# Gate and up products of a SwiGLU block with the weights stationary, in eight of eleven groups

## The chip, the cores and the metric

The program runs on one core of a Trainium2 chip. The time is that of one execution on the device, in microseconds (us). A core has five engines that matter here: TensorE (PE; the loads of its stationary operand are listed apart, as PEld), VectorE (DVE), ScalarE (ACT), GpSimd (POOL) and SyncE (SP), whose queue issues the DMAs. The metric is the median of several executions; the profile is of one further execution.

## The reference, cut to what matters

Two layers over 256 tokens of width 1024. Each layer is a feed-forward block (FFN), a mixer, and another FFN, each followed by a layer norm, in float32:

```python
def swiglu(x, w_gate, w_up, w_down):
    return (jax.nn.silu(x @ w_gate) * (x @ w_up)) @ w_down
...
for l in range(DEPTH):
    x = layer_norm(ALPHA * x + 0.5 * swiglu(x, ffn1_gate[l], ffn1_up[l], ffn1_down[l]), ln_g[l, 0], ln_b[l, 0])
    ...
    x = layer_norm(ALPHA * x + mix, ln_g[l, 1], ln_b[l, 1])
    x = layer_norm(ALPHA * x + 0.5 * swiglu(x, ffn2_gate[l], ffn2_up[l], ffn2_down[l]), ln_g[l, 2], ln_b[l, 2])
```

The hidden width of an FFN, `D_FF`, is 2816. There are four FFNs in all, and the change is in them.

## The kernel before, in words

**Precision.** A float32 operand is split into two float32r tiles, a high part (names ending in h) and the rest (ending in l): ScalarE casts, VectorE subtracts (`halves`, lines 101 and 102). A product is then three matmuls, high by high, high by low, low by high (`mm3`, lines 95 to 97), added up in one PSUM bank. In the profile a matmul is written `out<-moving,stationary`.

**Tiles.** The 256 tokens are two halves of 128 (`hf`). x of each half is kept transposed, as eight blocks of 128 by 128 (`xth`, `xtl`, one pair per half from a pool of three buffers), written by `Transposed.part` after a layer norm. The hidden width is cut into `NG` = 11 groups of `GW` = 256. The weights of a group come in four blocks of 128 by 1024, each holding two rows of blocks (kt) with 256 gate and 256 up columns, through two rings in SBUF: `w` with eight buffers and `x` with two. The down weights come in two blocks a group, through a ring `d` of six. A DMA brings each block as it is, `halves` splits it.

**One group.** `G(g, hf)` multiplies one half of the tokens with all weights of the group: x blocks are stationary, 512 weight columns move, 8 kt by 3 matmuls into one PSUM bank (`gu`), tokens on the partitions. `gate` takes silu of the gate columns on ScalarE (`sil`) and multiplies with the up columns on VectorE (`hn`). `T` transposes `hn`, two matmuls of 128 columns against the identity (line 355), and splits the result from PSUM into `hth` and `htl`. `D(g, hf)` multiplies these with the down weights: 4 `mm3` of 512 columns into two banks (`acc`) that add up over all eleven groups.

**Order.** TensorE's order is written out by hand: what is called first is recorded first. `T` is put off by a counter (`later`) that counts calls of `mm3`, six on from the gate, so that its two matmuls fall inside a later product; if `D` is called before its `T` was, `T` is recorded right there (`later.wait`). ScalarE, VectorE and GpSimd are ordered by a scheduler with priorities. `FFN.run` has the order:

```python
            for s in range(3, NG - 1):
                G(s, 0)
                D(s - 2, 1)
                G(s - 1, 1)
                D(s, 0)
            G(NG - 1, 0)
            G(NG - 2, 1)
            D(NG - 1, 0)
            G(NG - 1, 1)
```

Then follow D(8,1), D(9,1) and D(10,1). Weights are issued on SP in the order in which `Weight` objects are made, four blocks of gate and up for group g, then two of down for the same group; a buffer of a ring comes free when both halves have used it (`used`).

**Start.** The first FFN begins with seven matmuls of zeros (`WARM`, line 327) and has an order of its own for groups 0 and 1 (`start`, `pair`).

**Mixer.** It multiplies x with its input weights by the same `project`, builds its output transposed in two more pairs of the x pool (`mixed`), and multiplies those with `wout`.

Of the kernel before, what the change touches and what calls it, by code (L numbers as in the profile page):

```python
# [10 lines left out]
F32 = mybir.dt.float32  # L11
# [6 lines left out]
P = 128  # L18
# [19 lines left out]
RAW, NW, NX, ND = 5, 8, 2, 6  # L38
AHEAD, BEHIND = 100, 400
PINNED, STARTED = 4, 4  # L40
WARM = 7


class Later:
# [29 lines left out]
def trunk(ctx: ExitStack, tc: tile.TileContext, t, out: bass.AP):  # L74
# [3 lines left out]
    rawp = pool("raw", RAW)  # L78
    wp = pool("w", NW)
    xp = pool("x", 3)  # L80
    xtp = pool("xt", 3)
    sp = pool("small", 2)
    gbp = pool("gb", 1)
    psa = pool("psa", 4, space=PSUM)
# [82 lines left out]


    x, xT = [None, None], [None, None]

    class Transposed:
        def __init__(self, nat, slots=(), cuts=(0, 4, 8)):
            self.h = xtp.tile([P, KT, P], F32R, name="xth")
            self.l = xtp.tile([P, KT, P], F32R, name="xtl")
            self.nat, self.cuts, self.done = nat, list(cuts), 0
            for n in slots:
                later(n, self.part)
# [62 lines left out]
    def layer_norm(hf, accs, scale, gb, slots, last=False):  # L240
        z = xp.tile([P, D], F32, name="x")
        st = sp.tile([P, 2, 6], F32, name="st")
        mv = sp.tile([P, 2], F32, name="mv")
        rs = sp.tile([P, 1], F32, name="rs")
        for c in range(2):
            cs = slice(c * 512, c * 512 + 512)
            nc.vector.scalar_tensor_tensor(z[:, cs], accs[c], scale, x[hf][:, cs], ALU.mult, ALU.add)
            nc.vector.bn_stats(st[:, c, :], z[:, cs])
        nc.vector.bn_aggr(mv, st.rearrange("p a b -> p (a b)"))
        nc.vector.tensor_scalar_add(rs, mv[:, 1:2], LN_EPS / ALPHA ** 2)  # L250
        nc.gpsimd.tensor_tensor(rs, rs, neghalf[:, 0:1], ALU.pow)
        for c in range(2):
            cs = slice(c * 512, c * 512 + 512)
            nc.vector.scalar_tensor_tensor(z[:, cs], z[:, cs], mv[:, 0:1], gb[0][:, cs], ALU.subtract, ALU.mult)
            nc.vector.scalar_tensor_tensor(z[:, cs], z[:, cs], rs, gb[1][:, cs], ALU.mult, ALU.add)
            if last:
                nc.sync.dma_start(out[hf * P:(hf + 1) * P, cs], z[:, cs])
        x[hf] = z
        pinned[0] = PINNED
        if not last:  # L260
            xT[hf] = Transposed(z, slots)


    class FFN:
        def __init__(self, l, w, ln_i, first=False, last=False):
            gu, dn = t["gu"][l, w], t["dn"][l, w]
            self.first, self.last, self.mixer_next = first, last, not w
            self.slots = ((16, 18), (16, 18) if w else (13, 14))
            self.accs = [None, None]
            self.gw, self.dw, self.ht = {}, {}, {}  # L270
            self.ln = (l, ln_i)
            self.gb = None
            for g in range(NG):
                self.gw[g] = []
                for kq in range(4):
                    extra = (4 * g + kq) % (NW + NX) >= NW
                    self.gw[g].append(Weight(gu[g, kq], *(("x", NX) if extra else ("w", NW)),
                                             2 if first and g == 0 else 1))
                for n in {0: [], 1: [0, 1]}.get(g, [g]):
                    self.dw[n] = [Weight(dn[2 * n + i], "d", ND) for i in range(2)]  # L280

        def G(self, g, hf):
            ps = psg.tile([P, 2 * GW], F32, name="gu")
            project(hf, ps, self.gw[g])
            self.gate(g, hf, ps)

        def gate(self, g, hf, ps):
            sil = scope[0].tile([P, GW], F32, name="sil", bufs=2)
# [6 lines left out]
        def start(self):  # L295

            ws = self.gw[0]
            for w in ws:
                w.load()
            position[0] = STARTED  # L300
            pinned[0] = 6
            cuts = (0, 1, 2, 4, 6, 8)
            xr = [xp.tile([P, KT // 2, S], F32, name="x") for _ in range(2)]
            arrived = lambda a, b: xr[a // 4][:, a % 4:a % 4 + b - a, :]
            for a, b in zip(cuts, cuts[1:]):
                nc.sync.dma_start(arrived(a, b), t["xT"][:, a:b, :])
                for k in range(a, b):
                    ws[k // 2].fetch(k % 2)
            for hf in range(2):
                xT[hf] = Transposed(None, cuts=cuts)  # L310
            ps = [psa.tile([P, 2 * GW], F32, name="acc") for _ in range(2)]

            def split_x(n):
                a, b = cuts[n], cuts[n + 1]
                for hf in range(2):
                    halves(xT[hf].h[:, a:b, :], xT[hf].l[:, a:b, :], arrived(a, b)[:, :, hf * P:(hf + 1) * P])
                    xT[hf].done = b

            def multiply(kt):
                self.pair(kt, ws, ps)  # L320


            zero = scope[0].tile([P, 512], mybir.dt.bfloat16, name="zero")
            nc.vector.memset(zero, 0.0)
            idle = pst.tile([P, 512], F32, name="pt")
            for _ in range(WARM):
                nc.tensor.matmul(idle, zero[:, 0:P], zero, start=True, stop=True)
            with tc.manual_schedule(engines={mybir.EngineType.Activation, mybir.EngineType.DVE}):
                for what in "X0 W0 M0 X1 W1 M1 X2 W2 M2 W3 M3 X3 W4 M4 W5 M5 X4 W6 M6 W7 M7".split():
                    {"X": split_x, "W": lambda k: ws[k // 2].split(k % 2), "M": multiply}[what[0]](int(what[1]))  # L330
            for w in ws:
                w.uses = 0
            advance()
            for hf in range(2):
                self.gate(0, hf, ps[hf])
            ps = [psg.tile([P, 2 * GW], F32, name="gu") for _ in range(2)]
            for kt in range(KT):
                self.pair(kt, self.gw[1], ps)
                if kt % 2:
                    self.gw[1][kt // 2].uses = 0  # L340
                    advance()
            for hf in range(2):
                self.gate(1, hf, ps[hf])
# [8 lines left out]
        def T(self, g, hf, hn):  # L352
            pt = pst.tile([P, 2, P], F32, name="pt")
            for i in range(2):
                nc.tensor.transpose(pt[:, i, :], hn[:, i * P:(i + 1) * P], ident)  # L355
            hth = scope[0].tile([P, 2, P], F32R, name="hth", bufs=3)
            htl = scope[0].tile([P, 2, P], F32R, name="htl", bufs=3)
            with tc.high_priority(offset=AHEAD):
                halves(hth, htl, pt)
            self.ht[g, hf] = (hth, htl)  # L360

        def D(self, g, hf):
            later.wait(lambda: (g, hf) in self.ht)
            hth, htl = self.ht[g, hf]
            if g == 0:
                self.accs[hf] = [psa.tile([P, 512], F32, name="acc") for _ in range(2)]
            if g == 4 and hf == 0:
# [6 lines left out]
            for c in range(2):  # L374
                cs = slice(c * 512, c * 512 + 512)
                for i in range(2):
                    mm3(self.accs[hf][c], hth[:, i, :], htl[:, i, :], dw[i][0][:, cs], dw[i][1][:, cs],
                        g == 0 and i == 0, g == NG - 1 and i == 1)
            for w in self.dw[g]:
                w.used()  # L380
# [3 lines left out]
        def run(self):  # L384
            G, D = self.G, self.D
            if self.first:
                self.start()
                D(0, 0)
                D(0, 1)
                G(2, 0)  # L390
                D(1, 0)
            else:
                G(0, 0)
                G(1, 0)
                D(0, 0)
                G(0, 1)
                D(1, 0)
                G(2, 0)
                D(0, 1)
                G(1, 1)  # L400
            D(2, 0)
            for s in range(3, NG - 1):
                G(s, 0)
                D(s - 2, 1)
                G(s - 1, 1)
                D(s, 0)
            G(NG - 1, 0)
            G(NG - 2, 1)
            D(NG - 1, 0)
            G(NG - 1, 1)  # L410
            if self.mixer_next:
# [49 lines left out]
    def mixer(l, win, wout):  # L461
# [12 lines left out]
        kT, qT, A256, Pm, P01 = [None, None], [None, None], [None, None], [None, None], [None]  # L474

        def mixed(hf):
            mt[hf] = (xtp.tile([P, KT, P], F32R, name="xth"), xtp.tile([P, KT, P], F32R, name="xtl"))
            return mt[hf]

        def post_f(hf, ps):  # L480
# [231 lines left out]
        for hf in range(2):  # L712
# [5 lines left out]
            for n, kt in enumerate(WOUT_ORDER):  # L718
                later.wait(lambda: kt // 4 in ready[hf])
                wh, wl = wout[kt].parts  # L720
                for c in range(2):
                    cs = slice(c * 512, c * 512 + 512)
                    mm3(accs[c], mt[hf][0][:, kt, :], mt[hf][1][:, kt, :], wh[:, cs], wl[:, cs],
                        n == 0, n == KT - 1)
                wout[kt].used()
            layer_norm(hf, accs, 1.0 / ALPHA, gb, (15, 17) if hf else (13, 15))
        return guard

# [82 lines left out]
```

## Time and profile before

| | us |
|---|---|
| median of 3 runs | 975.86 (975.76 to 976.40) |
| the profiled execution, whole | 975.7 |
| its span, first to last instruction | 973.8 |
| TensorE busy in the span | 963.7 |
| VectorE busy | 622.6 |
| ScalarE busy | 480.0 |

The profile's page lists groups of instructions by line, with busy time, mean duration and the idle time ahead of them. The timeline lists single instructions with their start. A matmul's duration there includes its way through the array, so that the next one starts long before the listed end; the distance between two starts is what a matmul takes of the span.

### The profile page before, as it was taken

To read this page: it belongs to the slowest core of one execution; us is meant where nothing else is said; L and a number is where in the kernel's file an instruction comes from. 1 tells how busy PE (TensorE), PEld (TensorE's weight loads), DVE (VectorE), ACT (ScalarE), POOL (GpSimd) and SP (SyncE) were. 2 spreads that over 40 slices of the span, in tenths; PEclk is the share of its full clock that TensorE was granted. 3 is DMA by queue.
4 is the path that set the end of the run, shared out by engine and by line. 5 is a ranking of instruction groups with operands and counts; after the bars stand their busy time and mean duration, and the time that the engine had idled before them with its cause. 6 is when DMAs were issued, how large, how long until landed. Compare 5 with 4: busy or idle time off the path is not lost.

```text
span 973.8 us, 11992 instructions
## 1 busy us (share of the span) xinstructions
PE 963.7 (99%) x4423; PEld 791.5 (81%) x4423; DVE 622.6 (64%) x967; ACT 480.0 (49%) x682; POOL 26.5 (3%) x47
## 2 busy tenths in 40 slices
PE   9999999999999999999999999999999999999996
PEld 6788888888888888888888888888888888888885
DVE  6845554799779736454774645547897895645425
ACT  6735453467456535353543535343965464535320
POOL 0000000010010000000000000000001000000000
PEclk9999999999999999999999999999999999999999
DMA  8968646234436846546445564643345376564501
GB/s 289 331 222 302 237 161 227 94 114 172 145 117 224 296 170 237 196 163 225 137 165 217 187 245 154 234 142 131 128 132 159 107 266 248 189 243 156 212 1 43
DMA packets 51466, 180.58 MB, mean 185 GB/s; under 512 B 6096, under 2 KB 6352, under 8 KB 51408
## 3 DMA queue, kind: packets, MB, share of 16 engines
q1 hardware_dynamic: 51408, 179.83, 52.6%
q8 instruction: 34, 0.56, 0.2%
q14 instruction: 24, 0.20, 0.1%
HBM read 178.75 MB, written 1.05 MB: 185 GB/s over the span
## 4 chain that ended last, share of the span: by engine, by line
PE 99%; DVE 0%; DMA 0%; ACT 0%; issue 0%; DVEq 0%; SPq 0%
PE gu L97 20%; PE gu L95 20%; PE gu L96 20%; PE acc L97 10%; PE acc L95 10%; PE acc L96 10%; PE pt L355 2%; PE acc L595 2%; PE pt L183 1%; PE acc L567 1%; PE acc L568 1%; PE acc L631 0%; PE pt L692 0%; PE pt L510 0%; DMA raw<-in_gu 0%; PE acc L633 0%
## 5 line engine op out<-in xcount | busy, mean ns | idle before, releaser
L95 PE MATMUL gu<-wh,xth 128*128 128x512 f32 x720 | 289.5, 402 | 0.0
L97 PE MATMUL gu<-wh,xtl 128*128 128x512 f32 x720 | 282.1, 392 | 0.0
L96 PE MATMUL gu<-wl,xth 128*128 128x512 f32 x720 | 280.9, 390 | 0.0
L102 DVE TENSOR_TENSOR wl<-raw,wh 128x1024 fp32r<-128x1024 f32 (+1 forms) x204 | 242.7, 1200 | 18.5 <-ACT wh L101 12.8
L101 ACT CAST wh<-raw 128x1024 fp32r<-128x1024 f32 (+1 forms) x204 | 210.9, 1036 | 61.4 <-PE gu L97 44.6
L97 PEld LDWEIGHTS gu<-wh,xtl 128*128 128x128 f32 x720 | 135.1, 188 | 29.2
L96 PEld LDWEIGHTS gu<-wl,xth 128*128 128x128 f32 x720 | 135.8, 189 | 26.4
L95 PEld LDWEIGHTS gu<-wh,xth 128*128 128x128 f32 x720 | 135.4, 188 | 25.7
L102 DVE TENSOR_TENSOR dl<-raw,dh 128x1024 fp32r<-128x1024 f32 x88 | 104.4, 1222 | 74.2 <-ACT dh L101 74.0
L95 PE MATMUL acc<-dh,hth 128*128 128x512 f32 x352 | 138.9, 395 | 0.5 <-ACT hth L101 0.5
L97 PE MATMUL acc<-dh,htl 128*128 128x512 f32 x352 | 137.8, 391 | 0.0
L96 PE MATMUL acc<-dl,hth 128*128 128x512 f32 x352 | 137.4, 390 | 0.0
L101 ACT CAST dh<-raw 128x1024 fp32r<-128x1024 f32 x88 | 89.1, 1048 | 65.5 <-PE acc L97 50.7
L292 DVE TENSOR_TENSOR hn<-sil,gu 128x256 f32<-128x256 f32 x86 | 35.8, 418 | 125.9 <-ACT sil L291 125.8
L291 ACT ACTIVATE sil<-gu 128x256 f32<-128x256 f32 x86 | 33.1, 385 | 151.6 <-PE gu L97 151.4
L102 DVE TENSOR_TENSOR htl<-pt,hth 128x256 fp32r<-128x256 f32 x88 | 37.0, 421 | 83.6 <-ACT hth L101 83.5
L101 ACT CAST hth<-pt 128x256 fp32r<-128x256 f32 x88 | 32.4, 369 | 111.0 <-PE pt L355 110.9
L96 PEld LDWEIGHTS acc<-dl,hth 128*128 128x128 f32 x352 | 66.4, 189 | 14.1 <-DVE dl L102 0.4
L95 PEld LDWEIGHTS acc<-dh,hth 128*128 128x128 f32 x352 | 66.1, 188 | 14.3 <-ACT hth L101 0.7
L97 PEld LDWEIGHTS acc<-dh,htl 128*128 128x128 f32 x352 | 66.1, 188 | 14.3 <-DVE htl L102 0.4
L95 PE MATMUL gu<-xh,xth 128*128 128x512 f32 x128 | 52.3, 408 | 0.0
L97 PE MATMUL gu<-xh,xtl 128*128 128x512 f32 x128 | 50.6, 395 | 0.0
(136 smaller groups left out, 867.3 us busy)
## 6 DMA issues: line engine op xcount, KB each, us to landing
raw<-in_gu SPq DMA_DIRECT2D x172, 512.0 KB, 4.9
raw<-in_dn SPq DMA_DIRECT2D x88, 512.0 KB, 5.3
raw<-in_win SPq DMA_DIRECT2D x40, 512.0 KB, 4.5
raw<-in_wout SPq DMA_DIRECT2D x16, 512.0 KB, 4.3
lng<-in_ln_g SPq DMA_DIRECT2D x6, 512.0 KB, 5.1
lnb<-in_ln_b SPq DMA_DIRECT2D x6, 512.0 KB, 6.4
raw<-in_gu SPq DMA_DIRECT2D x8, 256.0 KB, 5.8
raw<-in_cumM SPq DMA_DIRECT2D x2, 512.0 KB, 7.6
```

What stands on the lines that cost most here:

```text
L95: nc.tensor.matmul(ps, lh, wh, start=start, stop=False)
L96: nc.tensor.matmul(ps, lh, wl, start=False, stop=False)
L97: nc.tensor.matmul(ps, ll, wh, start=False, stop=stop)
L101: first = nc.scalar.copy(dst_h, src)
L102: return first, nc.vector.tensor_tensor(dst_l, src, dst_h.bitcast(F32), ALU.subtract)
L183: nc.tensor.transpose(pt[:, k - a, :], self.nat[:, k * P:(k + 1) * P], ident)
L291: nc.scalar.activation(sil, ps[:, 0:GW], AF.Silu)
L292: nc.vector.tensor_tensor(hn, sil, ps[:, GW:2 * GW], ALU.mult)
L355: nc.tensor.transpose(pt[:, i, :], hn[:, i * P:(i + 1) * P], ident)
L567: nc.tensor.matmul(pe, lh[:, hs], cumM[:, hf, cs], start=True, stop=False)
L568: nc.tensor.matmul(pe, ll[:, hs], cumM[:, hf, cs], start=False, stop=True)
L595: nc.tensor.matmul(ps[B][0:rows, j, :], E[:, j, s0:s0 + rows], E[:, j, t0:t0 + ps[B].shape[2]], start=True, stop=True)
```

## The change

Groups 2 to 9 (`turned`) compute gate and up transposed. `G(g, n)` no longer means half n of the tokens but hidden columns n x 128 to n x 128 + 127 for all 256 tokens: a weight block of 128 by 128 is stationary and x of both halves moves, 256 columns. The product leaves with hidden columns on the partitions, which is how `D` needs it, so `gate_turned` makes `hth` and `htl` directly from SBUF and there is no `T`. For this both halves of x lie in one tile, whose two places the mixer swaps (`place`). Groups 0, 1 and 10 stay as they were.

```diff
+        def turned(self, g):
+            return 1 < g < NG - 1
+
+        def columns(self, kt, i, part, ps, ws):
+            wh, wl = ws[kt // 2].parts
+            xh, xl = xth[:, :, kt, :], xtl[:, :, kt, :]
+            o = ps[:, part * S:(part + 1) * S].rearrange("p (h t) -> p h t", h=2)
+            c = (kt % 2) * 512 + part * GW + i * P
+            lh, ll = wh[:, c:c + P], wl[:, c:c + P]
+            nc.tensor.matmul(o, lh, xh, start=kt == 0, stop=False)
+            nc.tensor.matmul(o, lh, xl, start=False, stop=False)
+            nc.tensor.matmul(o, ll, xh, start=False, stop=kt == KT - 1)
+            if kt % 2:
+                later.tick()
+
+        def gate_turned(self, g, i, ps):
...
+                nc.scalar.activation(sil, ps[:, 0:S], AF.Silu)
+                nc.vector.tensor_tensor(h, sil, ps[:, S:2 * S], ALU.mult)
+                halves(hth.rearrange("p h t -> p (h t)"), htl.rearrange("p h t -> p (h t)"), h)
+            self.ht[g, i] = (hth, htl)
...
-        def G(self, g, hf):
+        def G(self, g, n):
+            if self.turned(g):
+                ps = psg.tile([P, 2 * S], F32, name="gu")
+                for part in range(2):
+                    for kt in range(KT):
+                        later.wait(lambda: min(xT[0].done, xT[1].done) > kt)
+                        self.columns(kt, n, part, ps, self.gw[g])
+                        if kt % 2 and part:
+                            self.gw[g][kt // 2].used()
+                self.gate_turned(g, n, ps)
+                return
...
         def D(self, g, hf):
-            later.wait(lambda: (g, hf) in self.ht)
-            hth, htl = self.ht[g, hf]
+            if self.turned(g):
+                ht = [[p[:, place[hf], :] for p in self.ht[g, i]] for i in range(2)]
+            else:
+                later.wait(lambda: (g, hf) in self.ht)
+                ht = [[p[:, i, :] for p in self.ht[g, hf]] for i in range(2)]
...
-                for n in {0: [], 1: [0, 1]}.get(g, [g]):
+                for n in {0: [], 1: [0, 1], 2: [], NG - 1: [NG - 2, NG - 1]}.get(g, [g - 1]):
...
-            for s in range(3, NG - 1):
-                G(s, 0)
-                D(s - 2, 1)
-                G(s - 1, 1)
-                D(s, 0)
+            for g in range(3, NG - 1):
+                G(g, 0)
+                D(g - 1, 0)
+                G(g, 1)
+                if g < NG - 2:
+                    D(g - 1, 1)
             G(NG - 1, 0)
-            G(NG - 2, 1)
+            D(NG - 2, 0)
             D(NG - 1, 0)
             G(NG - 1, 1)
...
-WARM = 7
+HT = 6
+WARM = 14
...
-            zero = scope[0].tile([P, 512], mybir.dt.bfloat16, name="zero")
+            zero = scope[0].tile([P, 256], mybir.dt.bfloat16, name="zero")
...
-            hth = scope[0].tile([P, 2, P], F32R, name="hth", bufs=3)
-            htl = scope[0].tile([P, 2, P], F32R, name="htl", bufs=3)
+            hth = scope[0].tile([P, 2, P], F32R, name="hth", bufs=HT)
+            htl = scope[0].tile([P, 2, P], F32R, name="htl", bufs=HT)
...
-            self.h = xtp.tile([P, KT, P], F32R, name="xth")
-            self.l = xtp.tile([P, KT, P], F32R, name="xtl")
+            self.h, self.l = xth[:, place[hf]], xtl[:, place[hf]]
...
+            if hf == 0:
+                place.reverse()
```

In the groups that aren't turned the lines 95 to 97, 101 and 102 become 96 to 98, 102 and 103, and line 355 becomes 397. Within the first FFN groups 0 to 2 run as D(0,0), D(0,1), G(2,0), D(1,0), D(1,1), G(2,1); before, it was D(0,0), D(0,1), G(2,0), D(1,0), D(2,0). In the other FFNs the three groups run as G(0,0), G(1,0), D(0,0), G(0,1), D(1,0), G(1,1), D(0,1), G(2,0), D(1,1), G(2,1).

TensorE in the middle of an FFN, inside one G: `gu` is the product, `wh` and `wl` the weights, `xth` and `xtl` x transposed, `hn` the gated values of an earlier G. Before:

```order
L95 MATMUL gu<-wh,xth 128x512
L96 MATMUL gu<-wl,xth 128x512
L97 MATMUL gu<-wh,xtl 128x512
L355 MATMUL pt<-ident,hn 128x128 x2
L95 MATMUL gu<-wh,xth 128x512
```

and now, up to the down product that follows:

```order
L312 MATMUL gu<-xth,wh 128x256
L313 MATMUL gu<-xtl,wh 128x256
L314 MATMUL gu<-xth,wl 128x256
L96 MATMUL acc<-dh,hth 128x512
L97 MATMUL acc<-dl,hth 128x512
```

Each row of three stands 8 times in a G before and 16 times now, with the sides swapped and half the width, and no transposes stand between.

TensorE near the end of an FFN, where D(10,0) begins (`acc` the down product, `hth` the transposed gated values). Before, the transposes of G(10,0) stand inside G(9,1), whose last six rows lie between them and D(10,0):

```order
L355 MATMUL pt<-ident,hn 128x128 x2
L95 MATMUL gu<-xh,xth 128x512
L96 MATMUL gu<-xl,xth 128x512
L97 MATMUL gu<-xh,xtl 128x512
L95 MATMUL gu<-xh,xth 128x512
L96 MATMUL gu<-xl,xth 128x512
L97 MATMUL gu<-xh,xtl 128x512
L95 MATMUL acc<-dh,hth 128x512
```

and now they stand after the last row of D(9,0) and right ahead of the first of D(10,0):

```order
L97 MATMUL acc<-dl,hth 128x512
L98 MATMUL acc<-dh,htl 128x512
L397 MATMUL pt<-ident,hn 128x128 x2
L96 MATMUL acc<-dh,hth 128x512
L97 MATMUL acc<-dl,hth 128x512
```

G(9,1) has moved from there to before G(10,0), and D(9,0), which stood ahead of G(10,0), has taken its place.

More of the change, by code (lines that the diff above doesn't have):

```diff
@@ L80, in trunk @@
     xp = pool("x", 3)
-    xtp = pool("xt", 3)
+    xtp = pool("xt", 1)
     sp = pool("small", 2)
@@ L169, in trunk, with __init__ @@
     x, xT = [None, None], [None, None]
+    xth = xtp.tile([P, 2, KT, P], F32R, name="xth")
+    xtl = xtp.tile([P, 2, KT, P], F32R, name="xtl")
+    place = [0, 1]
     class Transposed:
-        def __init__(self, nat, slots=(), cuts=(0, 4, 8)):
-            self.h = xtp.tile([P, KT, P], F32R, name="xth")
-            self.l = xtp.tile([P, KT, P], F32R, name="xtl")
+        def __init__(self, hf, nat, slots=(), cuts=(0, 4, 8)):
+            self.h, self.l = xth[:, place[hf]], xtl[:, place[hf]]
             self.nat, self.cuts, self.done = nat, list(cuts), 0
@@ L260, in layer_norm @@
         if not last:
-            xT[hf] = Transposed(z, slots)
+            xT[hf] = Transposed(hf, z, slots)
     class FFN:
@@ L278, in __init__ @@
                                              2 if first and g == 0 else 1))
-                for n in {0: [], 1: [0, 1]}.get(g, [g]):
+                for n in {0: [], 1: [0, 1], 2: [], NG - 1: [NG - 2, NG - 1]}.get(g, [g - 1]):
                     self.dw[n] = [Weight(dn[2 * n + i], "d", ND) for i in range(2)]
-        def G(self, g, hf):
+        def G(self, g, n):
[9 more added lines that the diff above has]
+                return
+            hf = n
             ps = psg.tile([P, 2 * GW], F32, name="gu")
@@ L285, in G @@
             self.gate(g, hf, ps)
+        def turned(self, g):
[12 more added lines that the diff above has]
+        def gate_turned(self, g, i, ps):
+            sil = scope[0].tile([P, S], F32, name="sil", bufs=2)
+            h = scope[0].tile([P, S], F32, name="hn", bufs=2)
+            hth = scope[0].tile([P, 2, P], F32R, name="hth", bufs=HT)
+            htl = scope[0].tile([P, 2, P], F32R, name="htl", bufs=HT)
+            with tc.high_priority(offset=AHEAD):
+                nc.scalar.activation(sil, ps[:, 0:S], AF.Silu)
+                nc.vector.tensor_tensor(h, sil, ps[:, S:2 * S], ALU.mult)
+                halves(hth.rearrange("p h t -> p (h t)"), htl.rearrange("p h t -> p (h t)"), h)
+            self.ht[g, i] = (hth, htl)
         def gate(self, g, hf, ps):
@@ L309, in start @@
             for hf in range(2):
-                xT[hf] = Transposed(None, cuts=cuts)
+                xT[hf] = Transposed(hf, None, cuts=cuts)
             ps = [psa.tile([P, 2 * GW], F32, name="acc") for _ in range(2)]
@@ L320, in multiply @@
                 self.pair(kt, ws, ps)
-            zero = scope[0].tile([P, 512], mybir.dt.bfloat16, name="zero")
+            zero = scope[0].tile([P, 256], mybir.dt.bfloat16, name="zero")
             nc.vector.memset(zero, 0.0)
-            idle = pst.tile([P, 512], F32, name="pt")
+            idle = pst.tile([P, 256], F32, name="pt")
             for _ in range(WARM):
@@ L355, in T @@
                 nc.tensor.transpose(pt[:, i, :], hn[:, i * P:(i + 1) * P], ident)
-            hth = scope[0].tile([P, 2, P], F32R, name="hth", bufs=3)
-            htl = scope[0].tile([P, 2, P], F32R, name="htl", bufs=3)
+            hth = scope[0].tile([P, 2, P], F32R, name="hth", bufs=HT)
+            htl = scope[0].tile([P, 2, P], F32R, name="htl", bufs=HT)
             with tc.high_priority(offset=AHEAD):
@@ L376, in D @@
                 for i in range(2):
-                    mm3(self.accs[hf][c], hth[:, i, :], htl[:, i, :], dw[i][0][:, cs], dw[i][1][:, cs],
+                    mm3(self.accs[hf][c], ht[i][0], ht[i][1], dw[i][0][:, cs], dw[i][1][:, cs],
                         g == 0 and i == 0, g == NG - 1 and i == 1)
@@ L391, in run @@
                 D(1, 0)
+                D(1, 1)
+                G(2, 1)
             else:
@@ L397, in run @@
                 D(1, 0)
+                G(1, 1)
+                D(0, 1)
                 G(2, 0)
-                D(0, 1)
-                G(1, 1)
-            D(2, 0)
-            for s in range(3, NG - 1):
-                G(s, 0)
-                D(s - 2, 1)
-                G(s - 1, 1)
-                D(s, 0)
+                D(1, 1)
+                G(2, 1)
+            for g in range(3, NG - 1):
[4 more added lines that the diff above has]
+                    D(g - 1, 1)
             G(NG - 1, 0)
-            G(NG - 2, 1)
+            D(NG - 2, 0)
             D(NG - 1, 0)
@@ L476, in mixed @@
         def mixed(hf):
-            mt[hf] = (xtp.tile([P, KT, P], F32R, name="xth"), xtp.tile([P, KT, P], F32R, name="xtl"))
+            if hf:
+                mt[hf] = xth[:, place[0]], xtl[:, place[0]]
+            else:
+                mt[hf] = [xtp.tile([P, KT, P], F32R, name=n) for n in ("mth", "mtl")]
             return mt[hf]
```

## The prediction

> **What bounds the kernel now.** First the page: the engine totals, the chain of work that ended last, and one of the costliest groups; the transposes' row is from the view that groups instructions by line and shape.
>
> ```profile
> PE 963.7 (99%) x4423; PEld 791.5 (81%) x4423; DVE 622.6 (64%) x967; ACT 480.0 (49%) x682; POOL 26.5 (3%) x47
> ...
> PE 99%; DVE 0%; DMA 0%; ACT 0%; issue 0%; DVEq 0%; SPq 0%
> ...
> L101 ACT CAST wh<-raw 128x1024 fp32r<-128x1024 f32 (+1 forms) x204 | 210.9, 1036 | 61.4 <-PE gu L97 44.6
> ```
> ```profile
> L355 PE MATMUL pt<-ident,hn 128*128 128x128 f32 x176 | 33.3, 272 | 0.0
> ```
>
> TensorE is the chain: 99% of the span, and its 176 transposes had no idle time ahead of them either. The engines that split weights wait for it (of 61.4 us that ScalarE stood idle ahead of the weight casts, 44.6 ended when a gate/up matmul freed a buffer). So the time is a sum over TensorE's stream, and a matmul's duration isn't its price, because matmuls overlap. The price is the distance between two starts, read in the timeline: TensorE's matmuls (start and duration in us), then one of its weight loads.
>
> ```profile
> 648.88 0.39 PE L95 MATMUL gu<-wh,xth 128*128 128x512 f32 x1
> ...
> 654.09 0.39 PE L97 MATMUL gu<-wh,xtl 128*128 128x512 f32 x1
> 654.32 0.40 PE L95 MATMUL gu<-xh,xth 128*128 128x512 f32 x1
> ```
> ```profile
> 654.09 0.19 PEld L95 LDWEIGHTS gu<-xh,xth 128*128 128x128 f32 x1
> ```
>
> From 648.88 to 654.32 there are 24 distances: 5.44 / 24 = 0.2267 us for 512 columns. The load of the next stationary block starts with the running matmul and lasts 0.19 us, so it is hidden.
>
> One more pair of rows sets what the change must beat: the first matmul of a step's G(s,0), at 569.62 with its neighbours, and the same point four steps later. Each step is one gate/up product of each half, two down products and two pairs of transposes.
>
> ```profile
> 569.39 0.40 PE L97 MATMUL acc<-dh,htl 128*128 128x512 f32 x1
> 569.62 0.39 PE L95 MATMUL gu<-wh,xth 128*128 128x512 f32 x1
> 569.86 0.39 PE L96 MATMUL gu<-wl,xth 128*128 128x512 f32 x1
> ```
> ```profile
> 637.46 0.39 PE L95 MATMUL gu<-wh,xth 128*128 128x512 f32 x1
> ```
>
> (637.46 - 569.62) / 4 = 16.96 us for a group. It holds 48 gate/up and 24 down matmuls, 72 x 0.2267 = 16.32; the remaining 0.64 is transposes and what they disturb. One pair, in the timeline:
>
> ```profile
> 562.33 0.39 PE L97 MATMUL gu<-wh,xtl 128*128 128x512 f32 x1
> 562.56 0.38 PE L355 MATMUL pt<-ident,hn 128*128 128x128 f32 x2
> 562.70 0.48 PE L95 MATMUL gu<-wh,xth 128*128 128x512 f32 x1
> 563.01 0.39 PE L96 MATMUL gu<-wl,xth 128*128 128x512 f32 x1
> 563.24 0.40 PE L97 MATMUL gu<-wh,xtl 128*128 128x512 f32 x1
> 563.48 0.39 PE L95 MATMUL gu<-wh,xth 128*128 128x512 f32 x1
> ```
>
> From 562.33 to 563.01 pass 0.68 us where two matmuls alone take 0.45, so a pair costs 0.23 and two of them 0.46; the next distances, 0.23 and 0.24, add a little.
>
> **The change, part by part.** In 32 groups (8 of 11, in four FFNs) 48 matmuls of 512 columns become 96 of 256, each with a load of its own, and the two transpose pairs go. The columns streamed are the same. So everything hangs on one number that no row shows, the distance t between two 256-column matmuls of this type. Its bounds come from both sides.
>
> Below: the closest loads in this trace, the eight of line 631 (timeline of TensorE's loads, and the same eight in the chain of work).
>
> ```profile
> 256.52 1.09 PEld L631 LDWEIGHTS acc<-v,Pm 128*128 128x128 f32 x8
> ```
> ```profile
> 256.91 0.89 PE acc L631 x8
> ```
>
> Eight took 0.89 us, 0.111 each, though the view gives a single load 0.19: loads of full blocks overlap their own latency and can follow each other at 0.111. That is the lowest t the rows support.
>
> The columns themselves: at the start of the program the array is slow, and there the distances read as follows (timeline, then the row of the stretch with its granted clock, which says 1.00 all the same).
>
> ```profile
> 6.49 0.63 PE L97 MATMUL acc<-wh,xtl 128*128 128x512 f32 x1
> ...
> 8.20 0.63 PE L95 MATMUL acc<-wh,xth 128*128 128x512 f32 x1
> ```
> ```profile
> 5.00:9.00 4.00, 3.83 (x9) 2.78 (x10) 2.21 (x6) 1.99 (x7) 0.00 (x0) 1.00 0.84 243
> ```
>
> Four distances: (8.20 - 6.49) / 4 = 0.427, so at twice that pace 512 columns would take 0.2135. At full pace they take 0.2267: 0.0132 more than double pace accounts for. Either these 0.0132 belong to each matmul (they come with its load), and t = 0.1067 + 0.0132 = 0.120; or they belong to the columns, and t = 0.2267 / 2 = 0.1133. Which it is decides the sign. Rows that speak: the same matmul with another moving tile, blocks of the small x ring in place of w (timeline).
>
> ```profile
> 573.06 0.40 PE L97 MATMUL gu<-xh,xtl 128*128 128x512 f32 x1
> 573.30 0.39 PE L95 MATMUL gu<-xh,xth 128*128 128x512 f32 x1
> 573.53 0.40 PE L96 MATMUL gu<-xl,xth 128*128 128x512 f32 x1
> ...
> 574.93 0.40 PE L96 MATMUL gu<-xl,xth 128*128 128x512 f32 x1
> ```
>
> Here the distances alternate between 0.24 and 0.23, (574.93 - 573.06) / 8 = 0.234: same shape, same columns, 0.007 more. After a transpose pair, w blocks too are at 0.23 and 0.24 for some matmuls before they settle at 0.2267. A price of the columns would depend neither on which buffer holds them nor on what ran before. A collision of two readers, the moving stream and the load of the next block, would, and there is one load per matmul whatever its width. At the slow start the same loads cost nothing extra, as if the stream then had room. So I take **t = 0.120**; the upper end is the x ring's overhead at every matmul, 0.1067 + (0.234 - 0.2135) = 0.127.
>
> A rule of the Trainium skill speaks for the lower end: its page "TensorE: Matmul & The Clock Gate", Back-to-back issue gap, gives N / 2.4 + 2.5 ns, an estimated 0.109 for 256 columns; and under Part 2 it says that loading the next weights "doesn't steal SBUF read bandwidth from the running matmul". By that the whole sum would be near 947. Its 0.2158 for 512 columns isn't what the row shows (0.2267), so I don't take it at face value.
>
> Per group after: 96 x 0.120 = 11.52, the 24 down matmuls 24 x 0.2267 = 5.44, and 0.05 for four changes of accumulator at about 0.01 each (from 569.39 to 569.86 two distances take 0.47 in place of 0.453): 17.01. Against 16.96 that is +0.05, times 32 = **+1.6 us**. The transposes' 0.46 is eaten by 48 further loads at 0.0132 = 0.63.
>
> A new wait. At the end of each FFN, G(10,0) is followed by D(9,0) and D(10,0) at once. D(10,0) needs the transposed values of G(10,0), whose transposes are now recorded right ahead of it, with no matmuls between; before, six matmuls of G(9,1) stood there. Behind D(10,0) on TensorE stand G(10,1) and all that follows, so the wait is paid in full. The trace has one such place, in the first FFN, where transposes stand right ahead of D(1,0) (timeline of TensorE):
>
> ```profile
> 43.83 0.38 PE L355 MATMUL pt<-ident,hn 128*128 128x128 f32 x2
> 44.67 0.50 PE L95 MATMUL acc<-dh,hth 128*128 128x512 f32 x1 [0.46 <-ACT hth L101]
> ...
> 45.73 0.39 PE L95 MATMUL acc<-dh,hth 128*128 128x512 f32 x1
> ```
>
> Pair and three matmuls: 45.73 - 43.83 = 1.90, against 563.48 - 562.56 = 0.92 where the result isn't needed at once. So 0.98 each, four new ones, and that old one goes (G(2,0) now stands between): 3 x 0.98 = **+2.9 us**. Bounds: 0 if the cast and the subtraction come while D(9,0) still runs, 2 us each if ScalarE is in a weight cast of 1.04 us.
>
> Costed at nothing, by these rows (costliest groups; the last from VectorE's timeline).
>
> ```profile
> L102 DVE TENSOR_TENSOR wl<-raw,wh 128x1024 fp32r<-128x1024 f32 (+1 forms) x204 | 242.7, 1200 | 18.5 <-ACT wh L101 12.8
> ...
> L102 DVE TENSOR_TENSOR htl<-pt,hth 128x256 fp32r<-128x256 f32 x88 | 37.0, 421 | 83.6 <-ACT hth L101 83.5
> ```
> ```profile
> 182.65 0.69 DVE L427 TENSOR_TENSOR la<-raw 128x512 f32<-128x512 f32 x1 [1.41 <-DMA raw<-in_lb]
> ```
>
> The gate's chain keeps its four steps on ScalarE and VectorE, now from SBUF; D(g-1,0) wants the result only after the whole of G(g,0), 48 x 0.120 = 5.8 us later, and four steps like the one quoted (0.42) end in 1.7. A group's four weight blocks are all wanted in 24 matmuls (2.9 us) instead of 5.4, but the rings hold ten blocks for four a group, and the splitters wait for TensorE, as shown. Down weights are issued on SP one group later, and are read later by as much. The single x buffer and the swapped places put each new half where nothing is read any more. The warm-up is twice as many matmuls of half the width. Without that cover a late block of weights would cost one cast and one subtraction, 1.0 + 1.2 us; I put at most one such event in the first FFN. There too VectorE's line 427, which waited 1.41 us for a DMA, is now recorded ahead of G(10,0)'s product; D(9,0)'s 2.7 us cover that, else it costs up to 1.4 once.
>
> Sum, against the profiled execution's own 975.7 (span 973.8 and 1.9 around it; the median of the runs shown is 975.86): 975.7 + 1.6 + 2.9 = **980.2**, said as 980.
>
> **The rivals.**
> 1. The 0.0132 belong to the columns (t = 0.1133, still above the load floor of 0.111). Group: 10.88 + 5.49 = 16.37, -0.59, times 32 = -18.9, with the waits -16.0: **960**, faster. For it: 0.2267 is very steady over long stretches. Against it: buffer and history change the price, as shown. It wins from t below 0.1185, where 96 t + 5.49 + 0.09 = 16.96.
> 2. Load and stream now run side by side all the time, not for half a matmul, and collide as often as in the x ring: t = 0.127, group 12.19 + 5.49 = 17.68, +0.72, times 32 = +23.1, with the waits +26: **1002**. A quarter of the stationary blocks lie in the x ring, which had the worse distances as the moving side.
> 3. The load's whole 0.19 us becomes the distance: 96 x 0.19 + 5.49 = 23.73, +6.8 a group, +217 in all, +220 with the waits: **near 1195**. The rows of line 631 speak against it, with eight loads of this length in 0.89 us.
>
> Rival 3 is how far the Trainium skill's Best Practices (its page "Trainium Kernel Development and Optimization") would point, which judge headroom by the busy share of weight loads: 81% here, and twice the loads in the turned groups. The overlapping loads of line 631 are why I give it little.
>
> **How the numbers follow.** Forecast (t from 0.1165 to 0.1235) 0.53, rival 1 0.30, rival 2 0.13, rival 3 and the unforeseen 0.04. A measurement of this kernel tells apart about 0.2%, 1.95 us, which is t from 0.1179 to 0.1191: of the forecast's 0.53 I put 0.13 there, 0.03 below, 0.37 above. So faster 0.33, same 0.13, slower 0.54. The range takes in rivals 1 and most of 2: 957 to 1001, with some 0.08 left out below and 0.10 above. The forecast's own range is 969 to 991.
>
> **What would show it.** The distance between two matmuls of line 312 to 314 in the timeline: 0.120 (forecast), 0.113 (rival 1), 0.127 or alternating values (rival 2), 0.19 (rival 3). One group from start to start: 17.0, 16.4 or 17.7. At the end of each FFN an idle time on TensorE released by ScalarE's hth, about 0.5 us with a second gap for htl, four times. Transposes of line 397 at 48 instead of 176. If TensorE shows idle time ahead of line 312 released by weight casts, or if the busy share falls under 98%, the reading that only t and four waits matter was wrong.

## The result, and the profile after

| | before | after |
|---|---|---|
| median (us) | 975.81 (6 runs, 975.46 to 976.40) | 979.35 (6 runs, 977.97 to 980.55) |
| ratio, 95% interval | | 1.0036 (1.0023 to 1.0049) |
| profiled execution, and its span | 975.7, 973.8 | 979.2, 977.4 |

The change costs 3.5 us, 0.36%. From after's page: the engine totals, the chain that ended last, and one of the three new groups. From its view by lines and shapes: the transposes that are left.

```profile
PE 964.2 (99%) x5838; PEld 858.4 (88%) x5838; DVE 620.6 (63%) x967; ACT 474.5 (49%) x682; POOL 26.2 (3%) x47
...
PE 97%; DMA 1%; DVE 1%; ACT 0%; SPq 0%; issue 0%; DVEq 0%
...
L312 PE MATMUL gu<-xth,wh 128*128 128x256 f32 x768 | 217.3, 283 | 0.0
```
```profile
L397 PE MATMUL pt<-ident,hn 128*128 128x128 f32 x48 | 9.0, 273 | 0.2 <-DVE hn L334 0.2
```

TensorE still is the chain. It executes 1415 more matmuls (1536 gate/up more, 128 transposes fewer, 7 more in the warm-up), with the same busy time. The new matmuls never wait (0.0 idle ahead of 768). The 283 ns are a duration; the price is again the distance between two starts, in the timeline of TensorE (start, duration):

```profile
570.74 0.28 PE L314 MATMUL gu<-xth,wl 128*128 128x256 f32 x1
...
572.18 0.28 PE L314 MATMUL gu<-xth,wl 128*128 128x256 f32 x1
```

Twelve distances in 1.44 us: 0.120. For a group, six whole groups of the second FFN in both kernels (first matmul of a gate/up product at either end, before and then after):

```profile
356.11 0.39 PE L95 MATMUL gu<-wh,xth 128*128 128x512 f32 x1
...
457.78 0.39 PE L95 MATMUL gu<-wh,xth 128*128 128x512 f32 x1
```
```profile
354.69 0.28 PE L312 MATMUL gu<-xth,wh 128*128 128x256 f32 x1
...
456.55 0.28 PE L312 MATMUL gu<-xth,wh 128*128 128x256 f32 x1
```

101.67 / 6 = 16.945 before, 101.86 / 6 = 16.977 after: a group costs 0.03 more. The rest of the 3.5 us is elsewhere. After's waits of TensorE (what waited for what: us in total, times, longest), and before's of the same kind:

```profile
PE acc L96 <- ACT wh L102: 1.9, 3, 1.2
PE acc L96 <- ACT hth L102: 1.8, 4, 0.5
```
```profile
PE acc L95 <- ACT wh L101: 0.8, 1, 0.8
PE acc L95 <- ACT hth L101: 0.5, 1, 0.5
```

The four waits for `hth` are the forecast ones, D(10,0) at the end of each FFN. One of them, with the same pair of transposes and product for the other half twelve us later (TensorE's timeline), and the subtraction in VectorE's:

```profile
470.45 0.38 PE L397 MATMUL pt<-ident,hn 128*128 128x128 f32 x2
471.30 0.50 PE L96 MATMUL acc<-dh,hth 128*128 128x512 f32 x1 [0.46 <-ACT hth L102]
...
471.86 0.39 PE L98 MATMUL acc<-dh,htl 128*128 128x512 f32 x1
...
474.18 0.39 PE L96 MATMUL gu<-wh,xth 128*128 128x512 f32 x1
...
482.36 0.38 PE L397 MATMUL pt<-ident,hn 128*128 128x128 f32 x2
...
485.33 0.49 PE L186 MATMUL pt<-ident,x 128*128 128x128 f32 x3
```
```profile
471.27 0.42 DVE L103 TENSOR_TENSOR htl<-pt,hth 128x256 fp32r<-128x256 f32 x1 [2.45 <-ACT hth L102]
```

3.73 us with the wait, 2.97 without: 0.76 each. `htl` is ready at 471.69, just before the third matmul, so there is no second gap. The other waits stand at the very start, where line 96 waits for its first weights: the first matmul of G(2,0) starts at 35.55 before and 36.48 after.

```profile
35.55 0.39 PE L95 MATMUL gu<-xh,xth 128*128 128x512 f32 x1
```
```profile
36.48 0.28 PE L312 MATMUL gu<-xth,xh 128*128 128x256 f32 x1
```

So the span's +3.6 are: start +0.93; the first FFN's old stall gone, -1.0, and its transposes late by 0.35 behind VectorE's other work; four waits of 0.76, +3.0; and +0.3 that is left over, 0.07 for each FFN. Six turned groups alone are +0.19, so the rest of an FFN, its other two turned groups among it, is about 0.12 shorter than before. What shortens it is open.

### The profile page after: what moved, and what is told of

It is laid out like the page before. It is cut to its first block, busy times and chain, and to the rows that moved or that the text cites. A ratio compares the mean times of both kernels' runs of the same rounds, so it can differ in the third digit from the quotient of the medians.

```text
span 977.4 us, 14752 instructions
## 1 busy us (share of the span) xinstructions
PE 964.2 (99%) x5838; PEld 858.4 (88%) x5838; DVE 620.6 (63%) x967; ACT 474.5 (49%) x682; POOL 26.2 (3%) x47
## 4 chain that ended last, share of the span: by engine, by line
PE 97%; DMA 1%; DVE 1%; ACT 0%; SPq 0%; issue 0%; DVEq 0%
PE gu L314 13%; PE gu L312 12%; PE gu L313 12%; PE acc L96 10%; PE acc L97 10%; PE acc L98 10%; PE gu L96 8%; PE gu L98 8%; PE gu L97 8%; PE acc L648 2%; PE pt L186 1%; PE acc L620 1%; PE acc L621 1%; DMA x<-in_xT 1%; PE pt L397 1%; DMA raw<-in_lb 0%
## 5 line engine op out<-in xcount | busy, mean ns | idle before, releaser
L312 PE MATMUL gu<-xth,wh 128*128 128x256 f32 x768 | 217.3, 283 | 0.0
L314 PE MATMUL gu<-xth,wl 128*128 128x256 f32 x768 | 217.1, 283 | 0.0
L313 PE MATMUL gu<-xtl,wh 128*128 128x256 f32 x768 | 217.0, 283 | 0.0
L313 PEld LDWEIGHTS gu<-xtl,wh 128*128 128x128 f32 x768 | 147.0, 191 | 1.9
L312 PEld LDWEIGHTS gu<-xth,wh 128*128 128x128 f32 x768 | 146.7, 191 | 1.7
L314 PEld LDWEIGHTS gu<-xth,wl 128*128 128x128 f32 x768 | 146.8, 191 | 0.0
L96 PE MATMUL gu<-wh,xth 128*128 128x512 f32 x336 | 135.1, 402 | 0.0
L98 PE MATMUL gu<-wh,xtl 128*128 128x512 f32 x336 | 131.3, 391 | 0.0
L97 PE MATMUL gu<-wl,xth 128*128 128x512 f32 x336 | 130.9, 390 | 0.0
L97 PEld LDWEIGHTS gu<-wl,xth 128*128 128x128 f32 x336 | 63.3, 188 | 12.1
```

Of the source, the lines that this page charges most:

```text
L96: nc.tensor.matmul(ps, lh, wh, start=start, stop=False)
L97: nc.tensor.matmul(ps, lh, wl, start=False, stop=False)
L98: nc.tensor.matmul(ps, ll, wh, start=False, stop=stop)
L312: nc.tensor.matmul(o, lh, xh, start=kt == 0, stop=False)
L313: nc.tensor.matmul(o, lh, xl, start=False, stop=False)
L314: nc.tensor.matmul(o, ll, xh, start=False, stop=kt == KT - 1)
```

## The experiments

Three theories of the 256-column price were put against one another. **A**, the forecast's: some 0.013 us belong to each matmul with its load. **B**, rival 1: the price is that of the columns. **C**, added to A: what a matmul takes beyond its columns depends on where its stationary block lies in SBUF (the byte in its partition) relative to the moving tile.

**e1_streams**: a kernel of its own, which computes nothing of the reference. 32 equal matmuls in a row from one source line, each with its load; line by line another width or another place of the stationary block.

```diff
+    for n in range(REPS): mm(acc[:, 0:512], sta[:, 0:128], mov[:, 0:512], ...)
+    for n in range(REPS): mm(alt[:, 0:448], sta[:, 0:128], mov[:, 0:448], ...)
...
+    for n in range(REPS): mm(acc[:, 0:512], sta[:, 16:144], mov[:, 0:512], ...)
```

> A kernel of its own that computes none of the reference (it copies x to the output): streams of 32 equal matmuls on TensorE, one line each, of widths 512 down to 128, and of widths 512 and 256 with the stationary block shifted by 64 bytes a step against the moving one. Theory A (the overhead belongs to each matmul, with its load): with no shift the distance less 1/2400 us a column is about the same 0.013 us at 512, 448, 384, 320 and 256 (0.227, 0.200, 0.173, 0.147, 0.120), and from 192 down the load's floor of 0.111 us rules. Theory B (it belongs to the columns): 0.227, 0.198, 0.170, 0.142, 0.113. Theory C, a part of A (the overhead is a collision of load and stream in SBUF): the distance changes with the shift, within 0.216 to 0.240 at 512 and 0.111 to 0.127 at 256; if the load has nothing to do with places, no shift changes it.

From its timeline, where a stream is one row; the distance is (start of the next row - start) / 32. Lines 41 to 47 go down in width, line 49 is 512 columns with the block moved by 64 bytes, line 52 by 256, line 56 is 256 columns moved by 64.

```profile
42.76 7.42 PE L41 MATMUL acc<-mov,sta 128*128 128x512 f32 x32
50.01 6.65 PE L42 MATMUL alt<-mov,sta 128*128 128x448 f32 x32
56.49 5.73 PE L43 MATMUL acc<-mov,sta 128*128 128x384 f32 x32
62.07 4.85 PE L44 MATMUL alt<-mov,sta 128*128 128x320 f32 x32
66.75 4.00 PE L45 MATMUL acc<-mov,sta 128*128 128x256 f32 x32
70.59 3.72 PE L46 MATMUL alt<-mov,sta 128*128 128x192 f32 x32
74.14 3.71 PE L47 MATMUL acc<-mov,sta 128*128 128x128 f32 x32
77.69 4.05 PE L48 MATMUL alt<-mov,sta 128*128 128x256 f32 x32
81.57 7.63 PE L49 MATMUL acc<-mov,sta 128*128 128x512 f32 x32
89.04 7.58 PE L50 MATMUL alt<-mov,sta 128*128 128x512 f32 x32
...
103.79 7.44 PE L52 MATMUL alt<-mov,sta 128*128 128x512 f32 x32
111.06 7.62 PE L53 MATMUL acc<-mov,sta 128*128 128x512 f32 x32
...
133.30 3.80 PE L56 MATMUL alt<-mov,sta 128*128 128x256 f32 x32
136.94 3.95 PE L57 MATMUL acc<-mov,sta 128*128 128x256 f32 x32
```

| columns | 512 | 448 | 384 | 320 | 256 | 192 | 128 |
|---|---|---|---|---|---|---|---|
| distance (us) | 0.2266 | 0.2025 | 0.1744 | 0.1463 | 0.1200 | 0.1109 | 0.1109 |

Halving 512 to 256 saves 0.1066 and leaves 0.0134 that is not halved: theory A, where B asked for 0.1133. The widths between lie up to 0.0026 above the straight line of these two (at 448). At 192 and 128 columns the load floor of 0.111 rules. Line 48 is the change's own form, its 256 moving columns in two stretches of 128: 0.121 with no shift; it was not streamed at another place. And C: 512 columns take 0.2334 with the block 64 bytes further, 0.2272 at 256 bytes; 256 columns take 0.1138 at 64 bytes. The best place for one width is a bad one for the other.

**e2_split** and **e3_no_transposes** take the change apart. e2 is before with each gate/up matmul of groups 2 to 9 cut into two of 256 columns, the transposes kept. e3 is before with the transposes of groups 2 to 9 left out.

```diff
+        for c in range(2):
+            o = ps[:, c * 256:c * 256 + 256]
...
+                nc.tensor.matmul(o, xt.h[:, kt, :], wh[:, cs], start=kt == 0, stop=False)
```
```diff
-            pt = pst.tile([P, 2, P], F32, name="pt")
-            for i in range(2):
-                nc.tensor.transpose(pt[:, i, :], hn[:, i * P:(i + 1) * P], ident)
+            pt = hn.rearrange("p (i t) -> p i t", i=2)
+            if not 1 < g < NG - 1:
+                pt = pst.tile([P, 2, P], F32, name="pt")
...
```

> The kernel before, with the gate and up matmuls of groups 2 to 9 cut into two of 256 columns (twice the loads), transposes kept. Theory A: 32 groups x 48 further matmuls x 0.0132 us = +20 us, 996. Theory B: within 2 us of 975.8.

> The kernel before without the transposes of groups 2 to 9 (the down product takes the gated values as they are, so its output is another). Theory A and B alike: 64 transpose pairs fewer at 0.23 to 0.26 us each, -15 to -17 us, 959 to 961. If it gains clearly less, the transposes were partly hidden and the sum of the prediction was right by chance.

e2: 994.46, ratio 1.0191 (1.0176 to 1.0207), +18.8. e3: 960.19, ratio 0.9837 (0.9822 to 0.9852), -15.4. Six groups of the second FFN, in the timelines of e2 and of e3:

```profile
353.37 0.29 PE L197 MATMUL gu<-xh,xth 128*128 128x256 f32 x1
...
457.83 0.28 PE L197 MATMUL gu<-wh,xth 128*128 128x256 f32 x1
```
```profile
342.45 0.40 PE L95 MATMUL gu<-xh,xth 128*128 128x512 f32 x1
...
441.25 0.39 PE L95 MATMUL gu<-wh,xth 128*128 128x512 f32 x1
```

A group is 104.46 / 6 = 17.41 in e2 and 98.80 / 6 = 16.47 in e3, against 16.945. So 48 matmuls cut in two cost 0.465, 0.0097 for each further load, and two pairs of transposes cost 0.478, 0.239 a pair. The two cancel inside a group. (Times 32 e2's is 14.9; three waits for `htl`, 2.3 us idle in its waits, are part of the rest of the 18.8.)

**e4_tail** was to remove the four waits: after, with D(8,1) between D(9,0) and D(10,0).

```diff
             D(NG - 2, 0)
+            D(NG - 3, 1)
             D(NG - 1, 0)
...
-            for g in range(NG - 3, NG):
+            for g in range(NG - 2, NG):
```

> The changed kernel with D(8,1) put between D(9,0) and D(10,0) at the end of each FFN, so that the transposes of G(10,0) no longer stand right ahead of D(10,0). If the waits there are what the change adds besides its streams: four times 0.76 us and some 0.4 us in the first FFN less, -3.0 to -3.5, about 976. If the time doesn't move, the waits only shift something that is late anyway.

A miss: 989.75, ratio to before 1.0143 (1.0126 to 1.0160), 10 us slower than after. From its waits, then from TensorE's timeline at the start of the third FFN, and the row of a stretch there with its granted clock (0.50, third from the end):

```profile
PE gu L98 <- DVE xtl L103: 3.3, 3, 2.8
...
PE acc L96 <- ACT hth L102: 2.1, 4, 0.7
```
```profile
498.34 0.69 PE L98 MATMUL gu<-wh,xtl 128*128 128x512 f32 x1 [2.75 <-DVE xtl L103]
498.83 0.63 PE L96 MATMUL gu<-wh,xth 128*128 128x512 f32 x1
...
500.96 0.63 PE L98 MATMUL gu<-wh,xtl 128*128 128x512 f32 x1
```
```profile
498.60:501.80 3.20, 3.20 (x8) 2.48 (x8) 0.82 (x1) 0.00 (x0) 0.00 (x0) 0.50 0.47 106
```

D(8,1) had been covering what comes after it: the transposes of G(10,1), the layer norm and the transposes of x. The four waits for `hth` are still there, now ahead of D(10,1), and waits for x have come. Behind the longest of these the array also falls back: five distances from 498.83 to 500.96 are 0.43, the slow pace of the program's first microseconds, and the granted clock reads 0.50. This sets a reading of the prediction right: the 1.00 in its row of 5 to 9 us was no reading. In before's trace the record of the granted clock begins at 8.8 us, just where the distances turn to 0.23, and a stretch without a record is shown as 1.00.

**e6_tail_again** takes the cover from elsewhere: the loop stops a group earlier, then G(9,0), G(9,1), G(10,0), D(8,0), D(9,0), D(10,0), and D(8,1) stays at the end.

```diff
-            for g in range(3, NG - 1):
+            for g in range(3, NG - 2):
...
+            G(NG - 2, 0)
+            G(NG - 2, 1)
             G(NG - 1, 0)
+            D(NG - 3, 0)
```

> The changed kernel with G(10,0) moved up to right after G(9,1) and D(8,0) put behind it, so that D(8,0) and half of D(9,0) cover the way of G(10,0)'s values to D(10,0), and no down product of the second half is taken from the end of the FFN. If the waits ahead of D(10,0) are real and nothing else hides behind them: -3.0 to -3.5 us, about 976. If the end of the FFN is bound by the layer norm in any case, no change, or the wait turns up at the first transposes after it, as in the first try.

976.26 (11 runs), ratio to before 1.0003 (0.9995 to 1.0012): 3.1 less than after, and no wait for `hth` is left in its waits. Four waits of 0.76 are 3.0. Their price shows best in the second and the third FFN: from the first matmul of D(0,0) to the last of D(10,1) they take 176.29 and 176.36 us, in after 177.08 and 177.15, 0.79 more each. It is not all gain. Between these two FFNs TensorE now waits 0.65 for `xtl` and 0.18 for `xth`, and the way from the last down product of the one to the first of the other takes 13.15 us in place of 11.79.

**e5_streams2**: e1's kernel with other shifts.

```diff
+    for n in range(REPS): mm(acc[:, 0:512], sta[:, 60:188], mov[:, 0:512], ...)
...
```

> A second kernel of streams of its own, computing none of the reference: finer shifts of the stationary block at widths 512, 256 and 384, and 128 at three shifts. If the overhead is a collision of the load with the stream in SBUF, widths 512 and 256 each have their own best shift within the 256 bytes after which the first kernel's pattern repeated; at 256 the best is near the 0.1137 of a shift of 64 bytes, at 512 none is far below 0.2267, and at 128, where the load's floor of 0.111 rules, the shift changes nothing. If the 0.1137 was chance, the neighbours of 64 bytes read 0.118 to 0.120 like the rest.

At 512 columns 32, 96, 160 and 224 bytes give 0.233 to 0.234, 240 bytes 0.227 and 248 bytes 0.233: no smooth curve, and nothing under 0.2267. At 256 columns 64 bytes gives 0.114 again, every other shift tried 0.117 to 0.120; e1's 320 bytes gave 0.1181, so at this width the pattern does not simply repeat after 256 bytes. At 384 columns all lie between 0.173 and 0.177.

**e7_shift**: after, with 192 unused bytes ahead of x, so that the blocks of the large weight ring lie 64 bytes further from x than before (counted within 256 bytes). **e8_shift_and_tail**: e6 and e7 together.

```diff
+    pad = pool("pad", 1).tile([P, 48], F32, name="pad")
+    nc.gpsimd.memset(pad, 0.0)
     xtp = pool("xt", 1)
```

> The changed kernel with 192 bytes left free ahead of the x tiles, so that weight blocks of the large ring stand 64 bytes further than x within 256 bytes; nothing else moves. If the collision sets the distance: the 2304 turned matmuls with blocks of that ring go from 0.1196 to 0.1137 (-13.6 us), the 768 of the small ring stay near 0.118, the 1250 matmuls with x stationary and weights moving go from 0.2267 to 0.2289 (+2.7 us): -11, about 968, below both kernels. If the place in SBUF does nothing in the full kernel: 979.

> Both of the two before together. If they are independent: the sum of their gains, -14, about 965. If the gain of the shift is partly eaten by weights that now come late, less, with idle time on TensorE ahead of line 312 to 314.

e7: 970.90, ratio to before 0.9953 (0.9941 to 0.9965). e8: **967.33**, ratio 0.9913 (0.9900 to 0.9926), below both kernels of the case. The mean distance of a turned matmul, over all pairs of starts in the trace, falls from 0.1196 in after to 0.1164 in e7, not to the 0.114 of the stream. Two gate/up products of e8, each from one of its first matmuls to its last (TensorE's timeline):

```profile
569.23 0.28 PE L314 MATMUL gu<-xth,wh 128*128 128x256 f32 x1
...
574.77 0.28 PE L316 MATMUL gu<-xth,wl 128*128 128x256 f32 x1
```
```profile
594.42 0.28 PE L314 MATMUL gu<-xth,xh 128*128 128x256 f32 x1
...
595.84 0.28 PE L314 MATMUL gu<-xth,wh 128*128 128x256 f32 x1
...
599.80 0.28 PE L316 MATMUL gu<-xth,wl 128*128 128x256 f32 x1
```

The first runs at 5.54 / 47 = 0.118 throughout. The second begins with a block of the small ring, 12 distances of 0.118, and then takes 3.96 / 35 = 0.113 with the same kind of blocks that took 0.118 in the first. The same kind of tiles in the same places has two paces, and in this run the change from 0.118 to 0.113 always comes behind blocks of the small ring.

**e9_all_aligned** asked what picks the pace: e8 with the small ring and the down weights moved too (128 bytes left free at the far end of SBUF), so that all weight blocks stand 64 bytes from x, and with a warm-up of 19 x 192 columns. **e10_before_aligned** has the same 128 bytes in before alone, which brings its small ring level with x.

```diff
+    top = ctx.enter_context(tc.tile_pool(name="top", bufs=1, side="right")).tile([P, 32], F32, name="top")
+    nc.gpsimd.memset(top, 0.0)
     guard, scope[0] = scoped("ffn")
```

> The kernel of the shift and the tail together, with the small x ring, the down weights and the gated values moved by 128 bytes as well, so that every weight block stands 64 bytes from x, and the block loaded at each change from a down product to a turned one stands level with what then moves. (For room, the warm-up has 19 matmuls of 192 columns.) In the run before, turned products that began after a down product stayed at 0.118 and those that began with a block of the small ring went to 0.1137. If the distance depends on how a run of matmuls is entered, all go to 0.1137: another -7 to -8 us, about 960. If it depends on the ring's place alone, only the blocks of the small ring change, within 1 us of 967.

> The kernel before with the same 128 bytes left free at the far end, so that its small x ring stands level with x like the large one. If the collision is what makes its matmuls 0.234 and not 0.2267: 384 of them by 0.007, and the disturbed ones behind them, -2.5 to -4 us, about 972. If the small ring is slow for another reason, 976.

e9: 970.27, ratio to before 0.9941 (0.9927 to 0.9955), slower than e8. e10: 973.15, ratio 0.9970 (0.9958 to 0.9982), -2.8 against its before of 975.99. Two products of e9, the first of its turned ones and a later one, then the small ring's matmuls in e10 (timelines):

```profile
35.78 0.28 PE L314 MATMUL gu<-xth,xh 128*128 128x256 f32 x1
...
41.11 0.28 PE L316 MATMUL gu<-xth,wl 128*128 128x256 f32 x1
```
```profile
563.57 0.28 PE L314 MATMUL gu<-xth,wh 128*128 128x256 f32 x1
...
569.10 0.28 PE L316 MATMUL gu<-xth,wl 128*128 128x256 f32 x1
```
```profile
572.04 0.39 PE L97 MATMUL gu<-xh,xtl 128*128 128x512 f32 x1
...
573.40 0.39 PE L97 MATMUL gu<-xh,xtl 128*128 128x512 f32 x1
```

The later one runs at 5.53 / 47 = 0.118 with every block in the place that gave 0.1138 in the stream, and so do all others but one: a miss. The exception is the first, G(2,0) of the first FFN, which takes 5.33 / 47 = 0.113 from end to end in the same places. In e10 the small ring takes 1.36 / 6 = 0.227 instead of the 0.234 that the prediction read: place decides there, with not one instruction changed around it but a memset.

## Why the prediction was right

**The bound.** 980 was forecast and 979.35 measured, slower as forecast. The bound was right: TensorE's stream is the time, the groups' 0.03 and the waits add up on it, and the engines that split weights did not get in the way in the turned groups.

**t = 0.120, the step on which the sign hung.** Right in size and, for the larger part, in reason. With the prediction's 0.2135 for 512 columns, e1 leaves 0.0131 at 512 columns and 0.0133 at 256, so the overhead belongs to the matmul. This fells rival 1 as it was argued: it was to keep half of 0.0132. The reason given, a collision of stream and load, has this much behind it: moving tiles by bytes changes the distance, in e1, e5, e7 and e10. That all of the 0.013 is a collision is not shown; at 512 columns no place gave less than 0.2266. And 0.120 is the price where after's tiles happen to lie. With 192 bytes between, turned products run at 0.113 in part, which is rival 1's number, and e7 is below before. That the place was a dear one the prediction could not know, so the sign was in part luck.

**Rival 2.** Wrong in its mechanism: the small ring, dear as the moving side (0.234), is slightly cheap as the stationary side (0.119 in the mean of after). **Rival 3**: TensorE's busy share of loads rose from 81% to 88% and bounds nothing; loads of 0.19 us follow each other at 0.111 in e1's lines 46 and 47.

**The group.** 17.01 forecast, 16.98 measured. The prediction took all of the 0.64 beyond 72 x 0.2267 to be transposes and what they disturb. The transposes are 0.478 of it; e3, which has none in these groups, still holds 16.47 - 16.32 = 0.15. Some 0.09 of that would be the small ring's 12 matmuls at 0.007 more, an estimate. Turned groups lose the small ring's part as well, and so do those of e2, where both rings are at 0.121 in the mean, which is part of why 48 further loads come to 0.465 there and not to 0.63. So the sum held because t was right and the remainder was taken as a whole; its division was not right. What is left over in the four FFNs is +0.3 us, forecast +1.6.

**The waits.** Four, where forecast, 0.76 each instead of 0.98: the first gap is as in the row it was taken from (0.46), the second, for `htl`, isn't there, since VectorE was free sooner (2.45 us idle ahead of it). With the old stall gone and the late transposes in the first FFN that is +2.4, forecast +2.9. e6, without them, bears the price out, 0.79 in each of two FFNs. Line 427's "up to 1.4 once" came as 0.35.

**Costed at nothing.** Gate chain, down weights and the single x buffer held: no turned matmul waited. The start did not: +0.93 up to G(2,0). After's timeline there:

```profile
5.72 0.39 PE L98 MATMUL acc<-wh,xtl 128*128 128x512 f32 x1
...
10.39 0.50 PE L96 MATMUL acc<-wh,xth 128*128 128x512 f32 x1 [1.20 <-ACT wh L102]
```

In after the first matmuls already take the array's full pace (0.23 us from 5.72 to the next, against 0.427 before), and TensorE then stands waiting for ScalarE's `wh`, 1.20 us ahead of 10.39 and 1.9 in all. What makes it later on balance was not tried alone. The start of G(2,0) varies: 35.30 to 35.55 in before and the kernels made from it, 35.72 to 36.12 in those made from after. The early full pace is not the change's doing: e2, e4 and e7 begin slowly as before does, e3, e6, e8, e9 and e10 fast as after does.

So the sum came out closer than its terms. Groups and waits were forecast at +4.5 and came to +2.7, and 0.9 that was put at nothing made up half of the difference: that 980 and 979.35 lie so close is in part luck.

Two rules of the Trainium skill bear on the step that decided (page "TensorE: Matmul & The Clock Gate"). Its section Back-to-back issue gap gives N / 2.4 + 2.5 ns for a single matmul, which has the columns right (0.1066 for 256) but not the rest: 0.013 here, 0.007 at best. Under Part 2 it says that loading the next weights "doesn't steal SBUF read bandwidth from the running matmul"; for these operands the place of the two tiles moves the distance by 0.006 to 0.007, so the measurement speaks against it.

**Open.** Why one and the same kind of product runs at 0.113 or 0.118, and why in e9 only the first turned product ran at 0.113. The pace seems to be set by how a product is entered, but e9, which was to bring all to 0.113 by this, did not. Nor is it shown that 64 bytes are the best place for the change's own form, which was streamed with no shift alone.

## What to carry to other kernels

Swapping which operand is stationary keeps the columns streamed but changes the count of matmuls: price the fixed part of each (here 0.010 to 0.013 us) against what the swap removes, before writing it. In a hand-written order, a product that looks free to move may be the cover of a chain two steps later; e4 lost 10 us so, and e6 got 3 back by taking the cover from a place that had nearly enough to spare. When neighbouring matmuls differ in pace by 2 to 5% with the same shape, try where their tiles lie: 128 or 192 unused bytes were worth 2.8 us to before and 8.5 to after.

## What the runs showed of the hardware that was not expected

- The distance of two float32r matmuls is about 0.1066 us per 256 columns plus 0.0134, and 0.111 at 192 and at 128 columns (e1).
- The place of the stationary block relative to the moving tile changes it: 0.2266 to 0.234 at 512 columns, 0.1138 to 0.120 at 256, with different best places (e1, e5).
- At 256 columns the same kind of tiles in the same places can have two paces, 0.113 and 0.118, that hold for dozens of matmuls (e8, and in e9 one product against all others).
- After an idle stretch of 2.75 us, with shorter ones in the 12 us ahead of it, the granted clock was 0.50 for 3.4 us and 512 columns took 0.427 us (e4).
